# Three softmaxes queued as evacuations, paired transposes on TensorE, and rope in three products instead of four

## The chip, the cores and the metric

The kernel runs on one core of a Trainium2 chip. The metric is the device time of one execution in microseconds (us); of several executions the median is given. PE (TensorE), DVE (VectorE), ACT (ScalarE), POOL (GpSimd) and SP (SyncE, which issues the DMAs) each run their own instructions strictly in the order in which the program lists them, and wait on semaphores for one another.

## The reference, cut to what matters

One decoder layer over 256 tokens of width 1024. One input projection feeds two attention groups of 8 heads each (head size 64); their outputs go through one output projection; a SwiGLU feed-forward part (2816 hidden columns) and a gated per-layer embedding follow.

```
proj = rmsnorm(h) @ w_in
qa, ka, va, qi, ki, wi, qb, kb, vb = split(proj);  rope on qa, ka, qi, ki, qb, kb
B:  softmax(qb . kb / 8, causal) @ vb                      # 8 heads, own keys
A:  score = sum_h wi_h * relu(qi_h . ki);  keep the 64 highest keys of each query
    softmax(qa . ka / 8, causal and kept) @ va             # 8 heads, one shared key/value head
h = h + concat(A, B) @ w_out;   then feed-forward, embedding, final norm
rope(x) = [x1*cos - x2*sin, x2*cos + x1*sin]               # x1, x2: halves of a head
```

## The kernel before, in words

Tokens are two tiles of 128 (t = 0, 1). Every large product is made three times (`mm3`, `piece`) with operands cut into a rounded high part (`hi`) and a rest (`lo`); weights come in 1 MB chunks in a fixed order (`CHUNKS`). SP loads a chunk into a `raw` buffer, ACT rounds it into `hi` (L131, in two halves of 1024 columns), and DVE subtracts to get `lo` (L158, two halves). A chunk's `hi` buffer can be written once PE is done with the chunk three places earlier. Chunks 12 to 15 are the output projection (`w_out`), 16 and up the feed-forward part.

The stages up to the output projection are: column groups g0 to g4 of the input projection, `pp` (the embedding's small product), `wb` (the output projection's rows that belong to group B, 8 steps of 6 wide matmuls, for both token tiles) and `wa` (group A's rows, token tile 0, 4 steps). PE is scheduled by hand: it executes the matmuls in the order in which the code emits them, and the attention's small matmuls are dropped in between through a table: `at_tick(("wb", 3), ...)` emits its functions after step 3 of `wb`. A wide matmul here means one with 512 columns.

Attention is done in six units, `B[0..2]` and `A[0..2]`: `B[0]`, `A[0]` are token tile 0 with all 8 heads (128 keys); the others are token tile 1 with 4 heads each (256 keys). A unit has these steps:

- `qk`: PE makes the logits in two PSUM banks (e = 0, 1). Then the softmax, bank by bank: DVE adds the mask and takes the extremum (`lg`, `mn`, L465), ACT takes the exponential with a running sum (`pr`, L471), DVE inverts the sum (`rc`, L475) and multiplies (`pr`, L477).
- `tp(e)`: PE transposes `pr` of bank e, four 128x128 transposes (`pt`, L484); ACT copies the result (`pT`, L486).
- `pv`: PE multiplies by the values (L498); ACT and DVE write the result as `yH` and `yL` (L505, L506), the operands of the output projection.

Group A's mask `dmask` comes from `topk(t)`: DVE runs 8 rounds of MAX (`m8`, L428) and MATCH_REPLACE (L429) over the scores, each needing the one before, and writes the mask (L430, L431). `A[1]` and `A[2]` need the mask of t = 1, `A[0]` that of t = 0. All these small results share four PSUM banks (`aux`); a new one waits until the reader of the bank's former content is through.

`rope` (L323) is four DVE instructions on 8 heads: times cos (L326), the two half products with sin into `t2` (L327, L330), and the sum (L333). `evac_rope` calls it for qb, kb and qa of both tiles, `evac_g0` for the index and key parts.

DVE and ACT are ordered by the framework's list scheduler, which lays the instructions out ahead of time by priority. Code under `urgent()` (an offset of 100) is placed ahead of other ready work; before the change it holds the copies out of PSUM (L382, L486, L505, L506 and those after the attention). What the schedulers produce is a fixed order in each engine's queue; on the chip nothing overtakes.

## Time and profile before

| what | value |
|---|---|
| median of 3 runs | 330.67 us (330.64 to 331.22) |
| the profiled execution | 331.42 us, span of its instructions 329.6 us |
| PE, busy share of the span | 97% (320.2 us) |
| PE weight loads | 79% (260.9 us) |
| DVE | 71% (233.9 us) |
| ACT | 53% (175.8 us) |
| granted TensorE clock, mean | 0.997 |

The span runs from the first to the last instruction; the profiled execution's time is 1.8 us longer. A row of a timeline gives the start, the recorded duration, engine, line, operation, out<-in with buffer numbers left out (`pr_a` is any `pr` tile of an A unit) and, in brackets, how long the engine had been idle before it and who ended that. On DVE and ACT the next instruction usually starts some 0.08 to 0.1 us before the recorded end of the last, so the pace of a queue is read from differences of starts.

### The profile page before, as it was taken

To read this page: it belongs to the slowest core of one execution; us is meant where nothing else is said; L and a number is where in the kernel's file an instruction comes from. 1 tells how busy PE (TensorE), PEld (TensorE's weight loads), DVE (VectorE), ACT (ScalarE), POOL (GpSimd) and SP (SyncE) were. 2 spreads that over 40 slices of the span, in tenths; PEclk is the share of its full clock that TensorE was granted. 3 is DMA by queue.
4 is the path that set the end of the run, shared out by engine and by line. 5 is a ranking of instruction groups with operands and counts; after the bars stand their busy time and mean duration, and the time that the engine had idled before them with its cause. 6 is when DMAs were issued, how large, how long until landed. Compare 5 with 4: busy or idle time off the path is not lost.

```text
span 329.6 us, 4401 instructions
## 1 busy us (share of the span) xinstructions
PE 320.2 (97%) x1593; PEld 260.9 (79%) x1593; DVE 233.9 (71%) x476; ACT 175.8 (53%) x278; POOL 5.6 (2%) x16
## 2 busy tenths in 40 slices
PE   8999999899999999999999999999999999999991
PEld 8888887677777888888888888888878888888891
DVE  3979998999998697447745756467573525279884
ACT  4966456887577395334543455335534333338523
POOL 2001000000000000000000000000000000000110
PEclk9999999999999999999999999999999999999998
DMA  7995948420326146677568476675858564650011
GB/s 254 418 403 219 368 147 268 133 111 0 129 90 237 58 140 246 252 267 256 175 254 294 146 287 237 264 246 211 248 170 295 227 215 169 198 184 2 0 65 64
DMA packets 19029, 65.47 MB, mean 199 GB/s; under 512 B 3264, under 2 KB 8896, under 8 KB 12736
## 3 DMA queue, kind: packets, MB, share of 16 engines
q1 hardware_dynamic: 18864, 65.01, 55.7%
q8 instruction: 12, 0.20, 0.2%
q10 hardware_dynamic: 144, 0.20, 0.2%
q14 instruction: 9, 0.07, 0.1%
HBM read 61.26 MB, written 3.93 MB: 198 GB/s over the span
## 4 chain that ended last, share of the span: by engine, by line
PE 66%; DVE 18%; ACT 4%; issue 2%; ACTq 0%; DVEq 0%
PE ff L175 12%; PE ff L176 12%; PE ff L177 12%; PE wd L177 6%; PE wd L176 6%; PE wd L175 6%; DVE lo L158 5%; PE pg L177 2%; PE pg L175 2%; PE pg L176 2%; ACT hi L131 2%; DVE score L429 1%; DVE m L428 1%; DVE pr_a L477 1%; DVE pr_b L477 1%
## 5 line engine op out<-in xcount | busy, mean ns | idle before, releaser
L158 DVE TENSOR_TENSOR lo<-raw,hi 128x1024 fp32r<-128x1024 f32 (+1 forms) x99 | 116.7, 1206 | 59.5 <-ACT hi L131 59.5
L131 ACT CAST hi<-raw 128x1024 fp32r<-128x1024 f32 (+1 forms) x99 | 98.6, 1041 | 81.1 <-PE ff L177 37.3
L175 PE MATMUL ff<-hi,FH 128*128 128x512 f32 x176 | 68.7, 390 | 0.0
L177 PE MATMUL ff<-hi,FL 128*128 128x512 f32 x176 | 68.5, 389 | 0.0
L176 PE MATMUL ff<-lo,FH 128*128 128x512 f32 x176 | 68.5, 389 | 0.0
L177 PEld LDWEIGHTS ff<-hi,FL 128*128 128x128 f32 x176 | 33.0, 188 | 7.0
L175 PEld LDWEIGHTS ff<-hi,FH 128*128 128x128 f32 x176 | 33.0, 188 | 6.8
L176 PEld LDWEIGHTS ff<-lo,FH 128*128 128x128 f32 x176 | 33.0, 188 | 6.7
L177 PE MATMUL wd<-hi,hidL 128*128 128x512 f32 x88 | 35.1, 398 | 0.0
L175 PE MATMUL wd<-hi,hidH 128*128 128x512 f32 x88 | 34.8, 395 | 0.0
L176 PE MATMUL wd<-lo,hidH 128*128 128x512 f32 x88 | 34.7, 394 | 0.0
L312 PE MATMUL g<-hi,XH 128*128 128x512 f32 x64 | 25.8, 408 | 0.0
L312 PE MATMUL g<-hi,XL 128*128 128x512 f32 x64 | 24.9, 393 | 0.0
L312 PE MATMUL g<-lo,XH 128*128 128x512 f32 x56 | 21.6, 391 | 0.0
L176 PEld LDWEIGHTS wd<-lo,hidH 128*128 128x128 f32 x88 | 16.5, 188 | 4.2
L175 PEld LDWEIGHTS wd<-hi,hidH 128*128 128x128 f32 x88 | 16.5, 188 | 4.1 <-DVE hid L740 0.3
L177 PEld LDWEIGHTS wd<-hi,hidL 128*128 128x128 f32 x88 | 16.5, 188 | 3.8
L740 DVE SCALAR_TENSOR_TENSOR hid<-ff,f_y,sg 128x512 f32<-128x512 f32 (+1 forms) x12 | 8.4, 702 | 10.5 <-PE ff L177 9.4
L735 ACT ACTIVATE sg<-ff,f_y 128x512 f32<-128x512 f32 (+1 forms) x12 | 7.8, 648 | 15.0 <-PE ff L177 15.0
L312 PEld LDWEIGHTS g<-hi,XH 128*128 128x128 f32 x64 | 12.2, 190 | 3.0 <-issue 0.7
L312 PEld LDWEIGHTS g<-hi,XL 128*128 128x128 f32 x64 | 12.0, 188 | 2.7
L175 PE MATMUL pg<-hi,UH 128*128 128x512 f32 (+1 forms) x40 | 14.1, 352 | 0.0
(200 smaller groups left out, 445.1 us busy)
## 6 DMA issues: line engine op xcount, KB each, us to landing
raw<-in_w_dram SPq DMA_DIRECT2D x48, 1024.0 KB, 5.1
a<-in_xa_dram SPq DMA_DIRECT2D x8, 354.5 KB, 6.5
hidd<-hidb SPq DMA_DIRECT2D x10, 256.0 KB, 2.8
hidt<-hidd SPq DMA_DIRECT2D x40, 64.0 KB, 4.2
raw_g<-in_w_dram SPq DMA_DIRECT2D x2, 512.0 KB, 7.8
h<-in_x_dram SPq DMA_DIRECT2D x1, 1024.0 KB, 10.5
raw<-in_w_dram SPq DMA_DIRECT2D x2, 256.0 KB, 4.3
raw<-in_w_dram SPq DMA_DIRECT2D x1, 512.0 KB, 8.4
```

The costliest lines, as they stand in the source:

```text
L131: nc.scalar.copy(hi[:, o : o + step], raw[:, o : o + step])
L158: nc.vector.tensor_tensor(lo[:, o:e], raw[:, o:e], hi[:, o:e].bitcast(F32), op=ALU.subtract)
L175: nc.tensor.matmul(ps, aH, wH, start=start, stop=False)
L176: nc.tensor.matmul(ps, aH, wL, start=False, stop=False)
L177: nc.tensor.matmul(ps, aL, wH, start=False, stop=stop)
L312: nc.tensor.matmul(pss[t][:, :width], aT[:, k, tsl(t)], wT, start=k == 0 and n == 0, stop=k == KD - 1 and n == 2,)
L428: nc.vector.max(m8, s[:, :n])
L429: nc.vector.match_replace(s[:, :n], m8, s[:, :n], SENT)
L477: nc.vector.tensor_tensor(p3, p3, rc[:, je].unsqueeze(2).to_broadcast([P, nb, n]), op=ALU.mult)
L735: nc.scalar.activation(sg[:, :w], ps[:, :w], AF.Silu, scale=rf[t])
L740: nc.vector.scalar_tensor_tensor(hid[:, :w], up, rf[t], pgu[("s", t)][:, :w], op0=ALU.mult, op1=ALU.mult)
```

## The change

The softmax part of `Unit.qk` becomes a method of its own, and for `B[0]`, `A[0]` and `A[2]` it is recorded under `urgent()`; `B[1]`, `B[2]` and `A[1]` keep their normal priority. In the table, the two transposes of each unit are emitted one right behind the other, at the tick of the second or near it; other small groups are put next to each other too (`B[2].pv` beside `A[1].qk`). In `rope` the two half products become one instruction of 512 columns that reads the halves of each head in swapped order (a step of -32 elements).

```diff
--- before.py
+++ after.py
@@ -324,11 +324,11 @@
 
             t2 = a2.tile([P, 8, 64], F32, tag="rt2", name=f"{name}_t2")
             nc.vector.tensor_tensor(dst, src, tab[:, 0:64].unsqueeze(1).to_broadcast([P, nh, 64]), op=ALU.mult)
+            (ps, pn), (hs, hn), _ = src.ap
+            halves = bass.AP(src.tensor, src.offset + 32, [[ps, pn], [hs, hn], [-32, 2], [1, 32]])
             nc.vector.tensor_tensor(
-                t2[:, :nh, 0:32], src[:, :, 32:64], tab[:, 64:96].unsqueeze(1).to_broadcast([P, nh, 32]), op=ALU.mult
-            )
-            nc.vector.tensor_tensor(
-                t2[:, :nh, 32:64], src[:, :, 0:32], tab[:, 96:128].unsqueeze(1).to_broadcast([P, nh, 32]), op=ALU.mult
+                t2[:, :nh, :].rearrange("p h (r d) -> p h r d", r=2), halves,
+                tab[:, 64:128].rearrange("p (r d) -> p r d", r=2).unsqueeze(1).to_broadcast([P, nh, 2, 32]), op=ALU.mult,
             )
             nc.vector.tensor_tensor(dst, dst, t2[:, :nh, :], op=ALU.add)
 
@@ -450,6 +450,11 @@
                         else:
                             q, k = qbT[r, pair, tsl(t)], kbT[r, pair, 0:n]
                         nc.tensor.matmul(pss[e][:, i * n : (i + 1) * n], q, k, start=True, stop=True)
+                with urgent() if self in first else ExitStack():
+                    self.softmax(pss)
+
+            def softmax(self, pss):
+                t, n, nb = self.t, self.n, self.nb
                 mask = dmask[:, t, :n] if self.kind == "a" else cadd[:, 256 - n : 256]
                 self.pr = []
                 mn = sm.tile([P, 8], F32, tag="mn", name=f"mn_{self.name}", bufs=3)
@@ -510,40 +515,33 @@
         B = [Unit("b", t, h0) for t, h0 in ((0, 0), (1, 0), (1, 4))]
         A = [Unit("a", t, h0) for t, h0 in ((0, 0), (1, 0), (1, 4))]
 
+        first = (B[0], A[0], A[2])
+
         def at_tick(key, *fs):
             plan.setdefault(key, []).extend(fs)
 
         def tp(u, e):
             return lambda: u.tp(e)
 
-        at_tick(("g3", 2), lambda: tp_rope(1, 0, qbT))
-        at_tick(("g3", 3), lambda: tp_rope(1, 1, qbT))
-        at_tick(("g3", 4), lambda: tp_idx(0))
-        at_tick(("g3", 5), lambda: tp_idx(1))
+        at_tick(("g3", 3), lambda: tp_rope(1, 0, qbT), lambda: tp_rope(1, 1, qbT))
+        at_tick(("g3", 5), lambda: tp_idx(0), lambda: tp_idx(1))
         at_tick(("g3", 7), lambda: qk_idx(0))
         at_tick(("g4", 0), lambda: qk_idx(1), lambda: tp_rope(2, 0, kbT))
         at_tick(("g4", 1), lambda: tp_rope(2, 1, kbT))
         at_tick(("g4", 2), B[0].qk)
         at_tick(("g4", 3), B[1].qk)
-        at_tick(("g4", 5), tp(B[0], 0))
-        at_tick(("g4", 6), tp(B[0], 1))
-        at_tick(("g4", 6), B[2].qk)
+        at_tick(("g4", 6), tp(B[0], 0), tp(B[0], 1), B[2].qk)
         at_tick(("g4", 7), B[0].pv, lambda: topk(0))
-        at_tick(("pp", 0), tp(B[1], 0))
         at_tick(("pp", 0), lambda: topk(1))
-        at_tick(("pp", 1), tp(B[1], 1))
-        at_tick(("pp", 2), tp(B[2], 0))
-        at_tick(("pp", 3), B[1].pv, tp(B[2], 1), lambda: tp_rope(4, 0, qaT))
+        at_tick(("pp", 1), tp(B[1], 0), tp(B[1], 1))
+        at_tick(("pp", 3), B[1].pv, tp(B[2], 0), tp(B[2], 1), lambda: tp_rope(4, 0, qaT))
         at_tick(("wb", 0), A[0].qk, lambda: tp_rope(4, 1, qaT))
-        at_tick(("wb", 1), B[2].pv)
-        at_tick(("wb", 2), A[1].qk)
-        at_tick(("wb", 3), tp(A[0], 0))
-        at_tick(("wb", 4), tp(A[0], 1))
+        at_tick(("wb", 2), B[2].pv, A[1].qk)
+        at_tick(("wb", 4), tp(A[0], 0), tp(A[0], 1))
         at_tick(("wb", 5), A[0].pv, A[2].qk)
-        at_tick(("wb", 6), tp(A[1], 0))
-        at_tick(("wb", 7), tp(A[1], 1))
-        at_tick(("wa", 0), A[1].pv, tp(A[2], 0))
-        at_tick(("wa", 1), tp(A[2], 1))
+        at_tick(("wb", 7), tp(A[1], 0), tp(A[1], 1))
+        at_tick(("wa", 0), A[1].pv)
+        at_tick(("wa", 1), tp(A[2], 0), tp(A[2], 1))
         at_tick(("wa", 2), A[2].pv)
```

The orders below are those of the built programs; a name such as `pr_a101` is unit kind a, t = 1, first head 0, bank e = 1 (this is `A[1]`; `a00` is `A[0]`, `a14` is `A[2]`), followed by a buffer number. `wo` is the output projection, `lo14` a half of chunk 14's rest.

DVE, where `A[0]`'s first product stands among the rounds of the second top-k. Before:

```order
L475 RECIPROCAL rc_a00_993<-su_a00_992 128x4
L465 ISA lg_a001_1006,mn_a00_991<-qk_a001_982,dmask_257 128x128
L465 ISA mn_a00_991 128x1
L428 MAX m8_1_888<-score1_638 128x8
L477 TENSOR_TENSOR pr_a000_995<-pr_a000_995,rc_a00_993 128x512
L429 MATCH_REPLACE score1_638<-m8_1_888,score1_638 128x256
```

And after:

```order
L480 RECIPROCAL rc_a00_983<-su_a00_982 128x4
L429 MATCH_REPLACE score1_630<-m8_1_872,score1_630 128x256
L482 TENSOR_TENSOR pr_a000_985<-pr_a000_985,rc_a00_983 128x512
L428 MAX m8_1_872<-score1_630 128x8
L158 TENSOR_TENSOR lo14_1168<-raw14_860,hi14_862 128x1024
```

All eight mask additions of `A[0]` now stand ahead of this point, and both halves of chunk 14's subtraction stand among the rounds of the top-k (one just ahead of the eight, one here); before they stood behind the second mask.

DVE, where `A[1]`'s products (`pr_a100`, `pr_a101`) are made. Before:

```order
L475 RECIPROCAL rc_a10_1064<-su_a10_1063 128x2
L158 TENSOR_TENSOR lo14_1178<-raw14_870,hi14_872 128x1024
L477 TENSOR_TENSOR pr_a100_1066<-pr_a100_1066,rc_a10_1064 128x512
L475 RECIPROCAL rc_a10_1064<-su_a10_1063 128x2
L158 TENSOR_TENSOR lo14_1178<-raw14_870,hi14_872 128x1024
L477 TENSOR_TENSOR pr_a101_1074<-pr_a101_1074,rc_a10_1064 128x512
L158 TENSOR_TENSOR lo15_1209<-raw15_970,hi15_972 128x1024
L506 TENSOR_TENSOR yL_249<-pv_a00_1112,yH_248 128x4x128
```

And after, from the second inverse on:

```order
L480 RECIPROCAL rc_a10_1054<-su_a10_1053 128x2
L480 RECIPROCAL rc_a14_1121<-su_a14_1120 128x2
L158 TENSOR_TENSOR lo15_1193<-raw15_960,hi15_962 128x1024
L482 TENSOR_TENSOR pr_a140_1123<-pr_a140_1123,rc_a14_1121 128x512
L480 RECIPROCAL rc_a14_1121<-su_a14_1120 128x2
L482 TENSOR_TENSOR pr_a101_1064<-pr_a101_1064,rc_a10_1054 128x512
L482 TENSOR_TENSOR pr_a141_1131<-pr_a141_1131,rc_a14_1121 128x512
L158 TENSOR_TENSOR lo16_1328<-raw16_1021,hi16_1023 128x1024
```

`A[1]`'s second product now stands behind both halves of chunk 15's subtraction and behind `A[2]`'s mask additions, both of its inverses and its first product.

ACT, the exponentials of `A[1]` and the rounding of chunk 15. Before:

```order
L471 ACTIVATE pr_a100_1066,su_a10_1063<-lg_a100_1065,mn_a10_1062 128x256
L486 COPY pT_a00_1018<-pt_a000_1088 128x512
L471 ACTIVATE pr_a100_1066,su_a10_1063<-lg_a100_1065,mn_a10_1062 128x256
L471 ACTIVATE pr_a101_1074,su_a10_1063<-lg_a101_1073,mn_a10_1062 128x256 x2
L486 COPY pT_a00_1018<-pt_a001_1100 128x512
L131 CAST hi15_972<-raw15_970 128x1024 x2
L505 CAST yH_248<-pv_a00_1112 128x4x128
```

And after:

```order
L476 ACTIVATE pr_a100_1056,su_a10_1053<-lg_a100_1055,mn_a10_1052 128x256 x2
L131 CAST hi15_962<-raw15_960 128x1024
L510 CAST yH_248<-pv_a00_1102 128x4x128
L131 CAST hi15_962<-raw15_960 128x1024
L476 ACTIVATE pr_a101_1064,su_a10_1053<-lg_a101_1063,mn_a10_1052 128x256 x2
L476 ACTIVATE pr_a140_1123,su_a14_1120<-lg_a140_1122,mn_a14_1119 128x256 x2
L476 ACTIVATE pr_a141_1131,su_a14_1120<-lg_a141_1130,mn_a14_1119 128x256 x2
L131 CAST hi16_1023<-raw16_1021 128x1024
```

The exponentials of `pr_a101` moved behind both halves of chunk 15's rounding and the copy of `A[0]`'s result.

## The prediction

> **What bounds the kernel now.** I read the page's header and engine shares first, then the stretches around the attention, then PE's timeline for idle time in them.

> ```profile
> span 329.6 us, 4401 instructions
> PE 320.2 (97%) x1593; PEld 260.9 (79%) x1593; DVE 233.9 (71%) x476; ACT 175.8 (53%) x278; POOL 5.6 (2%) x16
> ...
> 80.00:92.00 12.00, 11.90 (x82) 8.69 (x79) 12.00 (x52) 7.76 (x27) 0.00 (x0) 1.00 0.26 89
> 92.00:105.00 13.00, 12.65 (x86) 9.54 (x86) 12.57 (x27) 10.13 (x24) 0.00 (x0) 1.00 0.48 163
> ```

> PE is busy for 97% of the span, so it is the bound as long as nothing holds it up. In the two stretches, which cover `wb` (busy time by engine in the order PE, PE's weight loads, DVE, ACT, POOL), DVE is busy for 12.00 of 12.00 and 12.57 of 13.00 us: there DVE is full, PE is nearly full, and who is late is a matter of a microsecond. PE's own timeline shows where it stood:

> ```profile
> 65.10 0.63 PE L484 MATMUL pt_b<-ident,pr_b 128*128 128x128 f32 x4 [0.83 <-DVE rc_b L475]
> ...
> 92.25 0.63 PE L484 MATMUL pt_a<-ident,pr_a 128*128 128x128 f32 x4 [0.35 <-DVE pr_a L477]
> ...
> 99.63 0.60 PE L484 MATMUL pt_a<-ident,pr_a 128*128 128x128 f32 x4
> ...
> 101.55 1.38 PE L498 MATMUL pv_a<-pT_a,va 128*64 128x128 f32 x16
> 102.86 0.66 PE L484 MATMUL pt_a<-ident,pr_a 128*128 128x128 f32 x4
> ...
> 105.27 0.63 PE L484 MATMUL pt_a<-ident,pr_a 128*128 128x128 f32 x4 [0.37 <-DVE pr_a L477]
> ```

> Three of these carry an idle time in brackets, all for transposes that waited for DVE: 0.83 (`B[0]`, bank 0), 0.35 (`A[0]`, bank 1), 0.37 (`A[2]`, bank 1). The fourth is hidden in a merged row: the `pv` of `A[1]` takes from 101.55 to 102.86, 1.31, where the same group elsewhere takes 1.02 (94.21 to 95.23, below), so it stood for 0.29. Together 1.84 us. That is all the time the change can free on PE by better timing. The row at 99.63 is `A[1]`'s bank 1: it has no idle time, its product was done long before. Remember it.

> **The change part by part.**

> *Pairs on PE.* Does a group of four transposes cost less beside another?

> ```profile
> 89.67 0.40 PE L177 MATMUL wo<-hi,yL 128*128 128x512 f32 x1
> 89.90 0.60 PE L484 MATMUL pt_a<-ident,pr_a 128*128 128x128 f32 x4
> 90.26 0.48 PE L175 MATMUL wo<-hi,yH 128*128 128x512 f32 x1
> 90.57 0.40 PE L176 MATMUL wo<-lo,yH 128*128 128x512 f32 x1
> ...
> 79.25 0.66 PE L484 MATMUL pt_b<-ident,pr_b 128*128 128x128 f32 x4
> 79.74 0.60 PE L380 MATMUL tr<-ident,qa 128*128 128x128 f32 x4
> ...
> 87.02 0.39 PE L177 MATMUL wo<-hi,yL 128*128 128x512 f32 x1
> 87.34 1.13 PE L452 MATMUL qk_a<-idxT,qaT 64*128 64x256 f32 x8
> 88.40 0.50 PE L175 MATMUL wo<-hi,yH 128*128 128x512 f32 x1
> 88.74 0.40 PE L176 MATMUL wo<-lo,yH 128*128 128x512 f32 x1
> ...
> 94.21 1.09 PE L498 MATMUL pv_a<-pT_a,va 128*64 128x128 f32 x16
> 95.23 1.13 PE L452 MATMUL qk_a<-idxT,qaT 64*128 64x256 f32 x8
> ```

> Alone between wide matmuls: 89.90 to the second wide one at 90.57 is 0.67; less one wide pace (89.67 to 89.90, 0.23) it is 0.44. Followed by another group (79.25 to 79.74) it takes 0.49. So two groups of transposes side by side save nothing. A small matmul group of another kind does pay at its borders: ahead of the `qk` at 87.34 the wide one took 0.32 instead of 0.23, and the first wide one behind it 0.34 (88.40 to 88.74). Between `pv` and `qk` side by side (94.21, 95.23) neither shows. The only new neighbours of that sort, `B[2].pv` and `A[1].qk`, save one of each: 0.09 + 0.10 = 0.19 us.

> *Rope.* Two halves become one instruction of 512 columns.

> ```profile
> L326 DVE TENSOR_TENSOR qa<-g,qcs 128x512 f32<-128x512 f32 x2 | 1.3, 672 | 0.0
> L327 DVE TENSOR_TENSOR qa_t<-g,qcs 128x256 f32<-128x256 f32 x2 | 0.8, 408 | 0.0
> ...
> 53.39 0.35 DVE L418 SCALAR_TENSOR_TENSOR score<-rel,w,init 128x128 f32<-128x128 f32 x1 [1.19 <-ACT rel L413]
> ```

> At the pace of the queue (recorded less 0.08) two halves take 2 x 0.33 = 0.66, one instruction of L326's size 0.59: 0.07 saved. No row has a source read with a step of -32. From below it costs what L326 costs, 0.59; from above I take twice that, 1.18. I take 0.59, the row of the same shape, sources and destination. Eight of the ten ropes stand ahead of 53.39, where DVE waits 1.19 us for ACT: they gain nothing. The two of `qa` stand in the full stretch: 0.14 gained, or at the upper end 1.0 lost.

> *The softmaxes given priority.* These only reorder DVE and ACT (SP's and POOL's queues keep their order), but a full queue has no free places: what goes ahead pushes something back. In the order of after, `A[0]`'s and `A[2]`'s softmaxes go ahead of `A[1]`'s, and so do chunk 14's and chunk 15's subtractions. I follow DVE with these rows:

> ```profile
> L158 DVE TENSOR_TENSOR lo<-raw,hi 128x1024 fp32r<-128x1024 f32 x10 | 12.1, 1216 | 0.6 <-ACT hi L131 0.6
> L428 DVE MAX8 m<-score 128x8 f32<-128x256 f32 x8 | 3.3, 418 | 0.0
> L465 DVE CUSTOM_DVE_ANT_0 lg_a<-qk_a,dmask 128x256 f32<-128x256 f32 x8 | 3.0, 414 | 0.0
> L465 DVE CUSTOM_DVE_ANT_0 lg_a<-qk_a,dmask 128x128 f32<-128x128 f32 x8 | 2.2, 276 | 0.0
> ...
> 80.29 0.27 DVE L431 TENSOR_TENSOR dmask<-dmask,cadd 128x128 f32<-128x128 f32 x1
> 80.48 0.09 DVE L429 MATCH_VALUE_LOAD score<-m,score 128x8 f32 x1
> ...
> 80.88 0.41 DVE L506 TENSOR_TENSOR yL<-pv_b,yH 128x256 fp32r<-128x256 f32 x1
> ...
> 89.75 0.42 DVE L431 TENSOR_TENSOR dmask<-dmask,cadd 128x256 f32<-128x256 f32 x1
> ...
> 95.46 0.68 DVE L477 TENSOR_TENSOR pr_a<-pr_a,rc_a 128x512 f32<-128x512 f32 x1
> ...
> 94.32 2.00 ACT L131 CAST hi<-raw 128x1024 fp32r<-128x1024 f32 x2 [0.44 <-PE wo L177]
> 96.22 0.58 ACT L505 CAST yH<-pv_a 128x512 fp32r<-128x512 f32 x1
> 98.31 0.51 ACT L471 ACTIVATE pr_a<-lg_a,mn_a 128x256 f32<-128x256 f32 x1 [1.51 <-DVE mn_a L465]
> ```

> Paces from them: a half chunk 1.13, MAX 0.34, MATCH_REPLACE with its load 0.40 (80.48 to 80.88), `lg` 0.35 or 0.21, a product 0.60, `yL` of 256 columns 0.33, a half chunk's rounding on ACT 0.95, `yH` 0.48, an exponential of 256 columns 0.50.

> First, the second mask (L431), which `A[1]` needs. Before: first mask done at 80.48, second at 89.75 + 0.34 = 90.1. After, the first is done some 0.5 earlier, at 80.0: one MAX fewer ahead of it and the two ropes. Between the masks there now stand 6 MAX (2.04), 6 MATCH_REPLACE (2.40), 4 half chunks (4.52), 2 `yL` (0.66), all 8 `lg` of `A[0]` (1.68), its 2 products (1.20), 2 inverses (0.2) and the mask itself (0.47): 13.2. I add 0.3 for ACT's first exponentials, which trail the eight `lg`, and 0.7 because the last three rounds of the top-k stand alone, each instruction waiting for the recorded end of the one before it (some 0.1 for each of seven; both are estimates from recorded less pace). Second mask at 80.0 + 14.2 = 94.2, 4 us later.

> Then `A[1]`. Its four `lg` end at 95.6. ACT takes bank 0's two exponentials (94.6 to 95.6), then half of chunk 15 (96.6), `yH` of `A[0]` (97.1), the other half (98.0), and only then bank 1's two (99.0) and `A[2]`'s first two (100.1 with the reading of the sum). DVE meanwhile: product of bank 0 (96.4), half of chunk 15 after ACT's half (97.8), `yL` (98.4), four `lg` of `A[2]` (99.8), the wait for `A[2]`'s sum (100.2), the other half (101.3), `A[2]`'s first product (101.9), an inverse, and `A[1]`'s second product, recorded end **102.7**. Before, that product started at 95.46.

> PE cannot go on with `A[1]`'s bank 1 before that. So the transposes of the row at 99.63 start at 102.7: 3.07 later. What PE has saved until then (the waits of 0.83 and 0.35, the 0.19) does not count, because it only lengthens this wait: PE gets there at about 99.2, after two short new waits of roughly 0.5 each. One is for `A[0]`'s bank 1, whose PSUM bank is freed by the `yL` of `B[2]`, now behind `A[0]`'s second product on DVE. The other is for the second bank of `A[2].qk`, which in the built program of after is the one that `A[1]`'s first `lg` have to empty; they run until 95. Then it stands for 3.5. Behind this point PE's work is the same as before, and the old waits of 0.29 and 0.37 are gone: `A[1].pv` comes 1.9 us after these transposes, enough for the copy behind half of chunk 16 on ACT (0.95 + 0.5), and `A[2]`'s products are ready at 103.4.

> The sum against the profiled execution: 331.42 + 3.07 - 0.29 - 0.37 = 333.8, that is +2.4. The median of the runs, 330.67, lies 0.75 under that execution, so I forecast 330.67 + 2.4 = **333.1 us**. My walk adds some 60 durations over 22.7 us; an error of 4% in it is 0.9 us, so this case by itself spans 332.2 to 334.0.

> What PE's clock makes of a wait of 3.5 us:

> ```profile
> 322.00:324.00 2.00, 0.67 (x6) 0.47 (x4) 1.18 (x4) 1.27 (x2) 0.00 (x0) 1.00 0.00 0
> 324.00:327.50 3.50, 0.00 (x0) 0.00 (x0) 1.65 (x6) 1.40 (x3) 0.00 (x0) 1.00 0.25 98
> 327.50:329.50 2.00, 0.00 (x0) 0.00 (x0) 0.00 (x0) 0.00 (x0) 0.00 (x0) 0.54 0.25 90
> ```

> PE is busy for the first 0.67 us of this tail and then no more; 4.8 us without a matmul pass with the granted clock at 1.00, and only the last stretch shows 0.54. So the sum keeps full clock through a wait of 3.5. [...]

> **Rivals.**

> 1. *It is faster: the priority takes the waits away and no new one comes.* For it: all four waits are for DVE or ACT work of attention units, and three of the four banks belong to units now ahead. Against it: `A[1]`'s second product. It decides at that product's end: if it is there by 99.2, PE saves 1.84 + 0.19 = 2.0 us, 328.6. That needs it 3.5 us earlier than the walk, with the order fixed.
> 2. *An even trade.* If the product ended at 99.63 + 0.66 = 100.3, the old waits behind it would pay for the new one: 330.7. The walk would have to be 2.4 us too long, or ACT's detour over chunk 15 be hidden.
> 3. *The swapped read of rope is slow.* Two `qa` ropes at the upper price put DVE back by 1.0 to 1.2 ahead of everything above: 334.2.
> 4. *PE's clock drops in the new wait.* Taking the slow stretch as long as the wait, 3.5 us of work at half rate cost 1.75: 334.9. For it: no wait of this length stands in the middle of the trace before. Against it: the tail, 4.8 us idle at full clock. [...]

> **How the numbers follow.** Forecast 0.70, faster 0.05, even 0.05, slow rope 0.08, clock 0.12. The range must leave out no more than 2 in 10: I leave out rivals 1 and 2 (0.10) and the outermost tails, and go from 332.1, a little under the forecast's lower end, to 335.0, which takes in rivals 3 and 4. About 0.2% (0.66 us) is what a measurement of this kernel can tell from no change. Slower by more than that are the forecast and rivals 3 and 4, 0.90; within it 0.05; faster 0.05.

> **What would show it.** Right: one idle time of about 3 to 4 us on PE ahead of a `pt_a` group near 102, ended by DVE's `pr_a`; no idle time at `pt_b` near 65 and none near 105; the second mask's row at about 94; half a chunk's `lo` and a product between `lg_a` and the late `pr_a`. The merged rope row near 0.67 us would settle rival 3, a granted clock of 1.00 in 100 to 110 rival 4. Wrong: a `pr_a` of `A[1]` that ends before 100, or wide matmuls that pace above 0.24 elsewhere, which my sum does not know of.

## The result and the profile after

The changed kernel takes 334.81 us (median of 6 runs, 332.96 to 336.04) against 330.75 for the kernel before: ratio 1.0114, 95% interval 1.0099 to 1.013. That is +4.1 us where +2.4 was forecast; it lies inside the range of 332.1 to 335.0, near its upper end. The profiled execution took 334.80 us, its span 332.9. One run of a later kernel, the one without `A[2]`'s priority, took 358.15 us at a mean clock of 0.851 and is left out of that kernel's median.

PE's list of waits (what waited, for what, us in total, times, longest) before, and the page's header, engine shares and the same list after:

```profile
PE warm L211 <- DVE wz L208: 1.0, 1, 1.0
PE pt_b L484 <- DVE rc_b L475: 0.8, 1, 0.8
PE pt_a L484 <- DVE pr_a L477: 0.7, 2, 0.4
```

```profile
span 332.9 us, 4387 instructions
...
PE 321.1 (96%) x1593; PEld 262.5 (79%) x1593; DVE 234.0 (70%) x466; ACT 174.7 (52%) x278; POOL 5.6 (2%) x16
...
PE pt_a L489 <- DVE pr_a L482: 3.3, 1, 3.3
PE warm L211 <- DVE wz L208: 1.0, 1, 1.0
PE qk_a L452 <- DVE mn_a L470: 0.4, 1, 0.4
PE pt_a L489 <- DVE yL L511: 0.3, 1, 0.3
```

The old waits at `pt_b` and `pt_a` are gone, and one of 3.3 us stands in their place, with two short ones ahead of it. (`warm` belongs to the start of the program, where both kernels are alike.) PE's timeline around the long one, after:

```profile
98.53 0.60 PE L489 MATMUL pt_a<-ident,pr_a 128*128 128x128 f32 x4
102.38 1.09 PE L489 MATMUL pt_a<-ident,pr_a 128*128 128x128 f32 x4 [3.26 <-DVE pr_a L482]
103.12 0.78 PE L175 MATMUL wo<-hi,yH 128*128 128x512 f32 x1
103.70 0.63 PE L176 MATMUL wo<-lo,yH 128*128 128x512 f32 x1
104.12 0.63 PE L177 MATMUL wo<-hi,yL 128*128 128x512 f32 x1
...
104.98 0.48 PE L176 MATMUL wo<-lo,yH 128*128 128x512 f32 x1
105.29 0.40 PE L177 MATMUL wo<-hi,yL 128*128 128x512 f32 x1
105.62 1.09 PE L503 MATMUL pv_a<-pT_a,va 128*64 128x128 f32 x16
```

The first row is `A[1]`'s bank 0, the second its bank 1: PE stood for 3.26 us until DVE's `pr_a`. Behind it the wide matmuls start 0.42 to 0.43 apart instead of 0.23 and are recorded at 0.63 instead of 0.40, up to about 105. The granted clock says why. Quarter microseconds in the order: length, PE, PE's weight loads, DVE, ACT, POOL, then clock, DMA share, GB/s:

```profile
101.50:101.75 0.25, 0.00 (x0) 0.00 (x0) 0.25 (x3) 0.25 (x2) 0.00 (x0) 0.94 0.00 0
101.75:102.00 0.25, 0.00 (x0) 0.00 (x0) 0.25 (x1) 0.25 (x2) 0.00 (x0) 0.50 0.00 0
...
105.00:105.25 0.25, 0.25 (x2) 0.25 (x1) 0.11 (x1) 0.00 (x0) 0.00 (x0) 0.73 0.25 98
105.25:105.50 0.25, 0.25 (x2) 0.00 (x0) 0.00 (x0) 0.00 (x0) 0.00 (x0) 1.00 0.09 33
```

The clock falls to 0.50 at 101.72 (0.94 means an eighth of that quarter at 0.50), while PE still waits, and comes back to 1.00 at 105.13, 3.41 us later. So two things cost time: the wait of 3.26 us, and the slow work behind it. DVE's timeline shows why the product came late, the second mask first:

```profile
93.18 0.42 DVE L431 TENSOR_TENSOR dmask<-dmask,cadd 128x256 f32<-128x256 f32 x1
...
95.54 0.69 DVE L482 TENSOR_TENSOR pr_a<-pr_a,rc_a 128x512 f32<-128x512 f32 x1
96.28 1.23 DVE L158 TENSOR_TENSOR lo<-raw,hi 128x1024 fp32r<-128x1024 f32 x1
...
99.77 1.20 DVE L158 TENSOR_TENSOR lo<-raw,hi 128x1024 fp32r<-128x1024 f32 x1
100.89 0.68 DVE L482 TENSOR_TENSOR pr_a<-pr_a,rc_a 128x512 f32<-128x512 f32 x1
101.49 0.16 DVE L480 RECIPROCAL rc_a<-su_a 128x2 f32<-128x2 f32 x1
101.57 1.27 DVE L482 TENSOR_TENSOR pr_a<-pr_a,rc_a 128x512 f32<-128x512 f32 x2
```

By the order, the product at 95.54 is `A[1]`'s first, the one at 100.89 is `A[2]`'s first, and the first of the two from 101.57 is `A[1]`'s second, on which PE waits. Before, it started at 95.46.

### The profile page after: what moved, and what is told of

Read it like the earlier page. It is cut to its first block, busy times and chain, and to the rows that moved or that the text cites. A ratio compares the mean times of both kernels' runs of the same rounds, so it can differ in the third digit from the quotient of the medians.

```text
span 332.9 us, 4387 instructions
## 1 busy us (share of the span) xinstructions
PE 321.1 (96%) x1593; PEld 262.5 (79%) x1593; DVE 234.0 (70%) x466; ACT 174.7 (52%) x278; POOL 5.6 (2%) x16
## 4 chain that ended last, share of the span: by engine, by line
PE 84%; DVE 9%; ACT 5%; issue 1%; DVEq 0%; ACTq 0%
PE g L312 14%; PE ff L177 12%; PE ff L175 12%; PE ff L176 12%; PE wd L175 6%; PE wd L177 6%; PE wd L176 6%; PE pg L177 2%; PE pg L175 2%; PE pg L176 2%; ACT pr_b L476 2%; DVE lo L158 2%; DVE score L429 2%; ACT hi L131 1%; ACT pr_a L476 1%; PE wo L175 1%
## 5 line engine op out<-in xcount | busy, mean ns | idle before, releaser
L158 DVE TENSOR_TENSOR lo<-raw,hi 128x1024 fp32r<-128x1024 f32 (+1 forms) x99 | 116.7, 1206 | 59.0 <-ACT hi L131 59.0
L131 ACT CAST hi<-raw 128x1024 fp32r<-128x1024 f32 (+1 forms) x99 | 98.6, 1041 | 80.0 <-PE wd L177 31.9
L175 PE MATMUL ff<-hi,FH 128*128 128x512 f32 x176 | 68.7, 390 | 0.0
L177 PE MATMUL ff<-hi,FL 128*128 128x512 f32 x176 | 68.5, 389 | 0.0
L176 PE MATMUL ff<-lo,FH 128*128 128x512 f32 x176 | 68.5, 389 | 0.0
L177 PEld LDWEIGHTS ff<-hi,FL 128*128 128x128 f32 x176 | 33.0, 188 | 7.0
L176 PEld LDWEIGHTS ff<-lo,FH 128*128 128x128 f32 x176 | 33.0, 188 | 6.9
L175 PEld LDWEIGHTS ff<-hi,FH 128*128 128x128 f32 x176 | 33.0, 188 | 6.7
L175 PE MATMUL wd<-hi,hidH 128*128 128x512 f32 x88 | 35.3, 402 | 0.0
L177 PE MATMUL wd<-hi,hidL 128*128 128x512 f32 x88 | 34.6, 394 | 0.0
L176 PE MATMUL wd<-lo,hidH 128*128 128x512 f32 x88 | 34.5, 393 | 0.0
L177 PEld LDWEIGHTS wd<-hi,hidL 128*128 128x128 f32 x88 | 16.5, 188 | 4.3
L175 PEld LDWEIGHTS wd<-hi,hidH 128*128 128x128 f32 x88 | 16.5, 188 | 4.0 <-DVE hid L738 0.3
L176 PEld LDWEIGHTS wd<-lo,hidH 128*128 128x128 f32 x88 | 16.5, 188 | 3.8
L175 PE MATMUL wo<-hi,yH 128*128 128x512 f32 x32 | 14.1, 442 | 0.0
```

Source lines behind the costliest of these rows:

```text
L131: nc.scalar.copy(hi[:, o : o + step], raw[:, o : o + step])
L158: nc.vector.tensor_tensor(lo[:, o:e], raw[:, o:e], hi[:, o:e].bitcast(F32), op=ALU.subtract)
L175: nc.tensor.matmul(ps, aH, wH, start=start, stop=False)
L176: nc.tensor.matmul(ps, aH, wL, start=False, stop=False)
L177: nc.tensor.matmul(ps, aL, wH, start=False, stop=stop)
```

## The experiments

My theory: the priority of `A[0]` and `A[2]` pushes `A[1]`'s second product behind chunk 15 and behind `A[2]`; PE waits for it, and the wait is long enough to drop the clock. Against it: the pairs cost the time, or the swapped read of rope, or the clock has another reason. All times below are medians against the kernel before on the same chip (331.0 to 331.2).

**Which part of the change does it?** Four kernels take it apart. The first is the kernel before with the priority alone:

```diff
+                with urgent() if self in first else ExitStack():
+                    self.softmax(pss)
...
+        first = (B[0], A[0], A[2])
```

> The kernel before with the priority for B[0], A[0] and A[2] alone; its table and its four-part rope stay. Late product (my theory: the priority puts A[1]'s second product behind chunk 15 and A[2], PE waits for it, and the wait lets the clock drop): a wait of 3 to 4 us on PE ahead of A[1]'s second transposes near 102 is still there; 333.0 to 333.5 us in runs that keep the clock, 334.8 to 335.3 in runs with one slow stretch. Rival (the pairs or the swapped read of rope cost the time): 330.7, no wait above 1 us.

Measured: 335.7 us (335.4 to 337.0), ratio 1.0144 (1.0126 to 1.0162), so the priority alone is at least as slow as the whole change. The long wait is there, but split: 1.12 us at the second bank of `A[2].qk`, 2.46 us at `A[1]`'s second transposes. PE's timeline, and its clock in stretches:

```profile
95.51 1.13 PE L452 MATMUL qk_a<-idxT,qaT 64*128 64x256 f32 x6 [1.12 <-DVE mn_a L470]
...
101.48 1.08 PE L489 MATMUL pt_a<-ident,pr_a 128*128 128x128 f32 x4 [2.46 <-ACT pr_a L476]
```

```profile
93.77:97.18 3.41, 2.29 (x11) 1.41 (x12) 3.22 (x11) 3.41 (x11) 0.00 (x0) 1.00 0.22 91
97.18:100.60 3.42, 1.84 (x5) 0.94 (x3) 3.37 (x13) 1.25 (x6) 0.00 (x0) 0.50 0.32 43
100.60:104.00 3.40, 2.52 (x8) 2.23 (x9) 2.60 (x7) 1.46 (x5) 0.00 (x0) 0.50 0.63 265
104.00:107.40 3.40, 3.40 (x11) 2.72 (x10) 1.16 (x1) 2.24 (x3) 0.00 (x0) 0.50 0.00 0
107.40:110.80 3.40, 3.40 (x29) 2.60 (x28) 1.71 (x3) 1.20 (x3) 0.00 (x0) 1.00 0.31 51
```

In this execution, the slowest of the four, the clock is at 0.50 from 97.16 to 107.40, 10.24 us or three times 3.41; its mean over the span is 0.981, over the four runs 0.981 to 0.991. The place of the wait was as expected, its size only with both waits taken together (3.58 us); the time is 0.4 us over the upper end. I had counted one slow stretch, and this execution had three. But one stretch of 3.41 us at 0.50 takes 3.41 x 0.5 / 333 = 0.005 off the mean clock, so by this estimate the runs at 0.989 and 0.991 had only one (kernels without a drop in the middle show 0.993 to 0.997), and they took 335.4 and 335.9 as well: what else the priority alone costs is open.

The second is the changed kernel without priority:

```diff
-        first = (B[0], A[0], A[2])
+        first = ()
```

> The changed kernel with no unit given priority; pairs and merged rope stay. Late product: no wait above 2 us near 102, clock 0.997, 330.0 to 331.5 us. Rival (pairs or rope cost it): 333 or more. Second rival (the pairs alone are a gain that the priority hid): 329.5 or less.

Measured: 331.5 us (330.8 to 332.3), ratio 1.0009 (0.9998 to 1.002): no change clear of the noise. Pairs and merged rope together neither cost nor gain. The third is the kernel before with the new table only, the fourth with the new rope only:

```diff
-        at_tick(("wb", 3), tp(A[0], 0))
-        at_tick(("wb", 4), tp(A[0], 1))
+        at_tick(("wb", 4), tp(A[0], 0), tp(A[0], 1))
...
```

> The kernel before with the paired table alone; priority and four-part rope as before. Late product: without priority A[1]'s second product is early, so no wait at A[1]'s second transposes; the pairs save 0.19 us and may shift short waits by up to a microsecond: 330.0 to 332.0 against 331.05, no wait above 2 us. Rival (pairs are what costs, since the first transposes of a pair now stand a step later and everything behind them too): 333 or more, with waits at pv.

```diff
+            halves = bass.AP(src.tensor, src.offset + 32, [[ps, pn], [hs, hn], [-32, 2], [1, 32]])
...
-                t2[:, :nh, 0:32], src[:, :, 32:64], tab[:, 64:96].unsqueeze(1).to_broadcast([P, nh, 32]), op=ALU.mult
...
-                t2[:, :nh, 32:64], src[:, :, 0:32], tab[:, 96:128].unsqueeze(1).to_broadcast([P, nh, 32]), op=ALU.mult
...
+                t2[:, :nh, :].rearrange("p h (r d) -> p h r d", r=2), halves,
...
```

> The kernel before with the merged rope alone. The merged row was 0.674 us for qa in the changed kernel against 0.408 + 0.406 for the two halves, so DVE is 0.14 us a pair of ropes ahead: 330.7 to 331.5, within 0.2% of before, unless the scheduler lays out the queues in another order. Rival (the swapped read of rope costs): 332 or more.

Measured: pairs alone 331.6 us, ratio 1.0017 (1.0008 to 1.0026); rope alone 331.9, ratio 1.0028 (1.0014 to 1.0042). Both a little slower, the second outside what I had expected. The timeline of its slowest run (333.8 us, with one slow stretch of the clock) shows no slow rope, but one wait at `B[0]`'s transposes that grew from 0.83 to 2.07. On DVE, two half chunks stand ahead of the inverse that these transposes need:

```profile
62.27 2.36 DVE L158 TENSOR_TENSOR lo<-raw,hi 128x1024 fp32r<-128x1024 f32 x2 [0.26 <-ACT hi L131]
...
65.78 0.79 PE L484 MATMUL pt_b<-ident,pr_b 128*128 128x128 f32 x4 [2.07 <-DVE rc_b L475]
```

With fewer instructions on DVE the scheduler laid the queues out anew. On DVE a second round of the first top-k and one more step of the scores now stand ahead of `B[0]`'s mask additions, which begin at 59.71 instead of 59.19; on ACT three of `B[0]`'s exponentials, where there had been two, stand ahead of the rounding of the next chunk. The half chunks wait for that rounding, as the bracket says, and start at 62.27 instead of 61.58, so the inverse behind them starts at 64.55 instead of 63.86, while PE gets there 0.6 earlier. The row of the merged instruction, in the changed kernel, is that of a product of its size:

```profile
L326 DVE TENSOR_TENSOR qa<-g,qcs 128x512 f32<-128x512 f32 x2 | 1.4, 676 | 0.0
L329 DVE TENSOR_TENSOR qa_t<-g,qcs 128x512 f32<-128x512 f32 x2 | 1.3, 674 | 0.0
```

**Which unit's place?** The changed kernel with `A[1]` given priority too, and with `A[2]` taken off:

```diff
-        first = (B[0], A[0], A[2])
+        first = (B[0], *A)
```

> The changed kernel with A[1] given priority too (B[0], A[0], A[1], A[2]). Late product: A[1]'s second product then stands ahead of chunk 15's second half and of A[2] again, the wait of 3.26 us at its transposes is gone; the two short waits of 0.34 and 0.37 ahead of it stay, and the pv of A[1] takes over a wait of 1 to 2 us, because ACT's copies of the transposes come later than PE: 331.0 to 331.8 us, clock mostly 0.994 or more. Rival (any unit given priority costs alike by what it pushes back): 333 or more.

```diff
-        first = (B[0], A[0], A[2])
+        first = (B[0], A[0])
```

> The changed kernel with priority for B[0] and A[0] alone. In its order A[1]'s second product is still behind ACT's two halves of chunk 15 and one half on DVE, but no longer behind A[2]'s inverses and first product and the second half. Late product, with both units ahead of A[1] to blame: some 2 us (1.13 for the half chunk, 0.60 for A[2]'s product, its inverse) come off the 3.26 us wait; about 1.2 us stays, and short waits at A[1]'s pv take back up to 1.1: 331.3 to 332.0, no drop of the clock in most runs. Rival (A[0]'s priority alone makes the late second mask and so the whole wait): 333 or more.

Measured: 331.6 us, ratio 1.0011 (1.0002 to 1.002), with `A[1]` ahead; 332.1 us, ratio 1.0028 (1.0016 to 1.004), without `A[2]`, just over the range that I gave. In the first, DVE makes `A[1]`'s second product at 96.72 and PE has no wait at its transposes, but one at its `pv`; in the second, DVE makes it at 99.45, and 0.84 us of the wait is left. The new waits of the two, in this order:

```profile
102.31 1.57 PE L503 MATMUL pv_a<-pT_a,va 128*64 128x128 f32 x16 [1.20 <-ACT pT_a L491]
```

```profile
100.28 0.63 PE L489 MATMUL pt_a<-ident,pr_a 128*128 128x128 f32 x4 [0.84 <-DVE rc_a L480]
103.38 1.09 PE L503 MATMUL pv_a<-pT_a,va 128*64 128x128 f32 x14 [0.71 <-ACT pT_a L491]
```

So the wait of 3.26 us has two parts: with `B[0]` and `A[0]` ahead the second mask is late (its row starts at 93.52 even without `A[2]`, at 88.98 without any priority), and `A[2]` ahead puts the one product that PE needs next behind work that it needs later. By the order of DVE's queue it is `A[0]`, whose softmax and both halves of chunk 14 stand among the rounds of the top-k; `B[0]` was not taken off alone, nor `A[2]` put ahead alone in this table. The third way is to leave the order alone and let PE ask later:

```diff
-        at_tick(("wb", 7), tp(A[1], 0), tp(A[1], 1))
-        at_tick(("wa", 0), A[1].pv)
-        at_tick(("wa", 1), tp(A[2], 0), tp(A[2], 1))
-        at_tick(("wa", 2), A[2].pv)
+        at_tick(("wa", 0), tp(A[1], 0))
+        at_tick(("wa", 1), tp(A[1], 1))
+        at_tick(("wa", 2), A[1].pv, tp(A[2], 0), tp(A[2], 1))
+        at_tick(("wa", 3), A[2].pv)
```

> The changed kernel with A[1]'s transposes put two steps of six wide matmuls later in the table (to the first two steps of wa, one each), its pv and A[2]'s transposes in the third step, A[2]'s pv in the fourth; priority, the other pairs and rope stay. Late product: two steps are 12 x 0.23 = 2.8 us of other work ahead of the wait, so 0.4 to 0.9 us of it is left, no clock drop (0.997), 330.1 to 330.7 us. Rival (the order on DVE costs PE time elsewhere, or pairs and rope do): 332 or more.

Measured: 330.5 us, ratio 0.9981 (0.9973 to 0.999), as expected. DVE's order is the same up to `A[2]`'s second product, and the transposes that wait for `A[1]`'s start no earlier (102.67, against 102.38), but PE has done 12 more wide matmuls by then:

```profile
102.67 0.63 PE L489 MATMUL pt_a<-ident,pr_a 128*128 128x128 f32 x4 [0.51 <-DVE pr_a L482]
```

**Is it the idle time that drops the clock?** The changed kernel with the wait filled by 12 idle wide matmuls, by 6 of them, and by 24 idle transposes, all into the PSUM bank that the real transposes then overwrite:

```diff
                 pt = aux(f"pt_{self.name}{e}")
+                if self is A[1] and e == 1:
+                    for _ in range(12):
+                        nc.tensor.matmul(pt, XH[:, 0, 0:P], XH[:, 0:2, :].rearrange("p k n -> p (k n)"), start=True, stop=True)
```

> The changed kernel with 12 idle matmuls of 512 columns ahead of A[1]'s second transposes, into the PSUM bank that these then overwrite: 12 x 0.23 = 2.8 us of the 3.26 us wait are filled, and nothing is moved. Late product plus clock: the transposes start at about 102.4 as in the changed kernel, the idle time ahead of them is under 0.8 us, the granted clock stays 1.00 from 100 to 108, the mean is 0.997 in all runs, and the time is that of the changed kernel's one run at 0.997, 333.0 us (+2.2 on before). Rival (the clock has no part, or drops for a reason other than idle time): 334.8, or slow wide matmuls at 103 to 105 though PE was busy.

> The changed kernel with 6 idle wide matmuls instead of 12 in the wait, so that 3.26 - 1.4 = 1.9 us of idle time stay. If the clock is decided over stretches of 3.4 us by the share of idle time, as the 2.07 us wait of the kernel with merged rope alone (slow clock in 2 of 12 runs) and the 1.50 us wait of the one with pairs alone (in none of 11) suggest: the clock stays in most runs, 333.3 to 333.7, and drops in at most one in four (335). If any wait at this place drops it: 334.8 to 335.3 in most runs.

```diff
                 pt = aux(f"pt_{self.name}{e}")
+                if self is A[1] and e == 1:
+                    for j in range(24):
+                        nc.tensor.transpose(pt[:, j % 4 * P : j % 4 * P + P], self.pr[0][:, j % 4 * P : j % 4 * P + P], ident)
```

> The changed kernel with the wait filled by 24 idle 128x128 float32 transposes instead of 12 wide matmuls: 24 x 0.11 = 2.6 us, into the bank that the real ones then overwrite. The real transposes start at about 102.4 as before. If any busy time of PE keeps the clock: 333.5 as with the wide matmuls, clock 0.993 to 0.997. If transposes count little as activity: the clock drops as in the changed kernel, 334.8 to 335.4, 0.991 or less, with wide matmuls at 0.43 behind them.

Measured: 333.5 us with 12 (332.9 to 333.7; ratio 1.0068, 1.0056 to 1.008), 0.5 over the 333.0 that I expected, 333.6 with 6 (332.9 to 334.8; 1.0076, 1.006 to 1.0092), 333.4 with transposes (333.0 to 334.0; 1.0067, 1.0055 to 1.0079). The changed kernel itself was run once more beside them, to see its spread:

> The changed kernel once more, to see how often its wait of 3.26 us drops the clock. If the clock is decided in stretches of 3.4 us that run on by themselves, a wait of 3.26 us fills most of one stretch in most runs and is split over two in the others: 334.8 to 335.3 at 0.991 or less in more than half of the runs, 333.0 to 333.7 at 0.993 to 0.997 in the rest. If the earlier spread came from the chip: all runs alike.

Measured: 334.7 us, ratio 1.0103 (1.0083 to 1.0124); five of its six runs have a mean clock of 0.988 to 0.992 and take 334.4 to 335.3, one has 0.997 and takes 332.9, as expected to within 0.4 us. The first six runs were alike: five at 0.984 to 0.991, one at 0.997 (332.96). In the profiled execution of the second six the clock is at 0.50 from 102.29 to 105.70, again 3.41 us. PE's timeline with 12 and with 6 matmuls in the wait:

```profile
98.98 3.02 PE L490 MATMUL pt_a<-XH 128*128 128x512 f32 x12
102.48 0.63 PE L492 MATMUL pt_a<-ident,pr_a 128*128 128x128 f32 x4 [0.48 <-DVE pr_a L482]
...
103.17 0.39 PE L176 MATMUL wo<-lo,yH 128*128 128x512 f32 x1
...
104.42 1.09 PE L506 MATMUL pv_a<-pT_a,va 128*64 128x128 f32 x16
```

```profile
98.35 1.64 PE L490 MATMUL pt_a<-XH 128*128 128x512 f32 x6
101.88 0.63 PE L492 MATMUL pt_a<-ident,pr_a 128*128 128x128 f32 x4 [1.89 <-DVE pr_a L482]
```

The real transposes start as late as in the changed kernel (with 6 matmuls PE's whole timeline between 68 and 112 lies 0.5 us earlier, and the transposes with it); nothing useful was done in the wait. But the wide matmuls behind it are recorded at 0.39 again. From the start of these transposes to the `pv` it is 1.94 us here (102.48 to 104.42) and 3.24 in the changed kernel (102.38 to 105.62): the stretch at 0.50 costs 1.3 us; the three fillings take 2.3 to 2.5 us more than the kernel before, and the changed kernel beside them 3.7. The mean clock is 0.993 to 0.996 with 12, not 0.997 as expected; the runs of the kernel before spread as much. With 6 matmuls, 1.9 us of idle time left, one run of six shows a drop (0.988, 334.79). Transposes kept the clock as well as wide matmuls did (0.993 to 0.997 in all five runs).

**A version that beats both.** It keeps pairs and merged rope, gives priority to `A[2]` alone, and moves some places of the table (of the rest only `topk(1)` and the transposes of qa and kb move, by one step):

```diff
-        first = (B[0], A[0], A[2])
+        first = (A[2],)
...
-        at_tick(("g4", 2), B[0].qk)
-        at_tick(("g4", 3), B[1].qk)
-        at_tick(("g4", 6), tp(B[0], 0), tp(B[0], 1), B[2].qk)
+        at_tick(("g4", 1), B[1].qk)
+        at_tick(("g4", 2), B[0].qk)
+        at_tick(("g4", 5), B[2].qk)
+        at_tick(("g4", 6), tp(B[0], 0), tp(B[0], 1))
...
-        at_tick(("g4", 7), B[0].pv, lambda: topk(0))
+        at_tick(("g4", 7), lambda: topk(0))
+        at_tick(("pp", 1), lambda: topk(1), tp(B[1], 0), tp(B[1], 1), B[0].pv)
+        at_tick(("wb", 0), A[0].qk, B[1].pv)
...
-        at_tick(("wa", 0), A[1].pv)
-        at_tick(("wa", 1), tp(A[2], 0), tp(A[2], 1))
+        at_tick(("wa", 0), tp(A[2], 0))
+        at_tick(("wa", 1), A[1].pv, tp(A[2], 1))
```

> A version meant to beat both: merged rope and pairs as in the changed kernel, priority for A[2] alone, and six places of the table moved: B[1].qk ahead of B[0].qk (a step earlier), B[2].qk a step earlier, B[0].pv two steps later and B[1].pv one, A[2]'s first transposes a step earlier and A[1].pv a step later, with topk(1) and the transposes of qa moved by one step. Late product: A[1]'s second product stays ahead of chunk 15's second half, no unit's products are pushed behind another's transposes, and no wait above 0.8 us is left on PE: about 1.2 to 2.0 us under before (the four waits of 1.84 and 0.19 for the borders): 329.0 to 329.8, clock 0.995 or more. Rival (what one unit gains another always loses while DVE is full): 331.

Measured: 329.2 us (328.5 to 329.3), ratio 0.9933 (0.9921 to 0.9945). On DVE the second mask now starts at 86.83 (89.75 before), and `A[1]`'s second product at 93.75 (95.46), ahead of both halves of chunk 15. Its timeline has one wait left between 60 and 112, and its PE is busy for 13.00 of the 13.00 us in which the kernel before was busy for 12.65. Which of its moves gains what was not taken apart:

```profile
90.64 0.63 PE L489 MATMUL pt_a<-ident,pr_a 128*128 128x128 f32 x4 [0.20 <-DVE rc_a L480]
```

```profile
92.00:105.00 13.00, 13.00 (x93) 9.77 (x93) 11.65 (x24) 9.24 (x20) 0.00 (x0) 1.00 0.45 163
```

**The waits against the times.** PE's recorded waits between 60 and 112 us of each profiled execution (one for each kernel), and the median time:

| kernel | waits on PE, us | less before's 1.84 | time against before, us |
|---|---|---|---|
| best version | 0.20 | -1.64 | -2.1 |
| asked later | 0.34 + 0.37 + 0.51 = 1.22 | -0.62 | -0.5 |
| no priority | 0.38 + 0.49 + 0.99 = 1.86 | 0.0 | +0.5 |
| pairs alone | 1.50 + 0.91 = 2.41 | +0.6 | +0.6 |
| without `A[2]` | 0.34 + 0.38 + 0.84 + 0.71 = 2.27 | +0.4 | +0.9 |
| `A[1]` ahead too | 0.36 + 0.38 + 1.20 = 1.94, and 0.48 inside the pv row (1.57 for 1.09) | +0.6 | +0.5 |
| rope alone | 2.07 + 0.23 + 0.38 = 2.68, and 0.28 inside the pv row (1.37 for 1.09) | +1.1 | +0.8 |
| changed kernel | 0.34 + 0.37 + 3.26 = 3.97 | +2.1 | +2.2 at full clock, +4.1 median |
| priority alone | 1.12 + 2.46 = 3.58 | +1.7 | +4.6 |

Down to the last two rows the sum of PE's waits gives the time within 0.5 us. In those two a second term appears. In the changed kernel it is the clock; with the priority alone the slow stretches are part of it, and the rest is open.

## Why the prediction was right, point by point

- **The place and the cause of the new wait: right.** One wait ahead of `A[1]`'s second transposes, 3.26 us where 3.5 was forecast, ended at 102.38 where 102.7 was. Nothing at `pt_b` near 65, nothing near 105. The two short ones ahead of it were 0.34 and 0.37, not 0.5 each.
- **The walk on DVE: right in length, its start off.** First mask at 79.4, second at 93.6: 14.2 us between them, as walked; both 0.6 earlier than said, since the first top-k ended 1.1 us earlier than before and not 0.5. The row of the first mask starts at 79.14 here and at 79.30 without priority, so that is not the priority's doing. Some of that was given back: the transposes behind the second product started only 0.3 early.
- **The sum: right without the clock.** +2.4 was forecast; the two runs at a mean clock of 0.997 show +2.2 and +1.9, the kernel with the wait filled +2.5, the one filled with transposes +2.3. The waits came to +2.1 (3.97 against 1.84); with the 1.3 us of the clock that is the 3.4 by which the two profiled executions differ (334.80 and 331.42). The median's +4.1 holds another 0.7 us only because the kernel before was profiled in an execution 0.7 above its median and the changed kernel was not.
- **Pairs: right.** Eight transposes and what follows take 1.10 us from their start to the second wide matmul (108.14 to 109.24 in the changed kernel), less one pace 0.87; two groups alone are 2 x 0.44. Without priority the changed kernel stands at 1.0009.
- **Rope: right on the price** (674 ns, no dearer for its swapped read). What I did not count is that fewer instructions also move the scheduler's order: rope alone came out 0.28% slower through another wait.
- **The clock: the step that failed.** "So the sum keeps full clock through a wait of 3.5" was read from the tail, where 4.8 us without a matmul passed at 1.00. In 10 of 12 runs of the changed kernel the clock fell (means of 0.984 to 0.992, where the other two have 0.997); that adds 1.3 us where it falls for one stretch and makes the median +4.1 (+3.7 in the second six). I had it as a rival at 0.12 and 1.75 us. That 334.81 lies in the range is owed to that rival and the one on rope: for them the upper end was put at 335.0, while the forecast by itself spanned 332.2 to 334.0 and missed. That the rival's 334.9 is so near is partly luck, since its 1.75 stood for 1.3 and the forecast's 2.4 for waits of 2.1, and the 0.7 of the medians made up for it. No run shows the 1.75, half of the wait: the slow stretch took 3.41 us behind the wait of 3.26 and behind the one of 2.07 (rope alone), and 1.3 is what it cost in the changed kernel. The tail was one observation; why the clock fell in ten runs of the changed kernel and not in two is not shown.

## What to carry to other kernels

Priority on a full in-order queue moved lateness here and removed none: given alone, it turned 1.84 us of waits on PE into 3.58. Before giving it, write down in which order the bound engine will ask for the results, and never put a unit that is asked for later ahead of one that is asked for sooner. If a result has to be late, let the bound engine ask later instead (same order on DVE, 330.5 us here instead of 334.8). And count a wait on TensorE as long as those here twice: for itself, and for the stretch at half clock that may follow it, as it did here (3.41 us at 0.50 in the traces; after a wait of 1.9 us in 1 of 6 runs, after 2.07 in 2 of 12, after 3.26 in 10 of 12), or fill it with idle matmuls, which took 1.2 to 1.4 us off here.

## What the runs showed of the hardware

```profile
330.00:331.00 1.00, 0.00 (x0) 0.00 (x0) 0.00 (x0) 0.00 (x0) 0.00 (x0) 0.71 1.00 383
```

A mean of 0.71 means 0.58 of that microsecond at 0.50, so the drop is at 330.42, which is 228.7 us behind the first one at 101.72, or 67 times 3.413. That fits stretches that run on by themselves, as I supposed ahead of the second six runs; but it is one distance in one execution and proves nothing of the others.

The stretch ahead of each drop and the slow one (changed kernel; rope alone), and the two ahead of the drop in the tail of the kernel before:

```profile
98.33:101.74 3.41, 0.80 (x6) 0.46 (x4) 3.28 (x14) 3.41 (x12) 0.00 (x0) 1.00 0.00 0
101.74:105.12 3.38, 2.74 (x9) 2.38 (x10) 3.37 (x4) 1.84 (x3) 0.00 (x0) 0.50 0.86 305
```

```profile
62.71:66.12 3.41, 1.34 (x8) 0.87 (x7) 3.41 (x10) 3.00 (x14) 0.00 (x0) 1.00 0.16 19
```

```profile
324.24:327.65 3.41, 0.00 (x0) 0.00 (x0) 1.44 (x5) 1.16 (x3) 0.00 (x0) 1.00 0.30 115
320.83:324.24 3.41, 1.84 (x16) 1.64 (x14) 2.49 (x8) 1.51 (x2) 0.00 (x0) 1.00 0.00 0
```

PE was busy for 0.80 and for 1.34 of the 3.41 us ahead of these two drops, and for 2.29 ahead of the one with the priority alone, some 1.7 of them with `qk`. In the tail of the kernel before, the stretch from 320.83 held 1.84 us of work and the one from 324.24 none, and the clock stayed at 1.00 through both: 5.0 us without a matmul passed there ahead of the drop (322.67 to 327.65), where 2.6 were enough in the changed kernel (99.13, where the transposes end, to 101.72). So neither the idle time ahead of a drop nor the work in the 3.41 us ahead of it is enough to tell these cases apart: 1.84 us of work were followed by full clock, 2.29 by half. Whether `qk` counts for less than other matmuls was not tried.

The waits, and the runs whose mean clock shows a drop (0.992 or less): 1.50 us, none of 11 (pairs alone, all at 0.993 or more); 1.9 us, one of 6 (0.988); 2.07 us, 2 of 12 (rope alone, 0.990 and 0.991); 3.26 us, 10 of 12 (0.984 to 0.992).

With the priority alone the stretches at 0.50 in which PE was busy for 1.84 and 2.52 us were followed by another at 0.50, and the one with 3.40 by full clock, as the one with 2.74 was in the changed kernel. These figures can't be set beside those at full clock, since a wide matmul is recorded at 0.63 us at 0.50 and at 0.40 at 1.00.
